# Attention's last group of a two-layer diffusion block: context tokens first, four output weights rounded ahead, and pieces of the output projection between scores and transposes

## The chip, the core and the metric

The kernel runs on one core of one Trainium2 chip. A core has a tensor engine (PE, matrix products), a vector engine (DVE), a scalar engine (ACT), GpSimd (POOL) and a queue for transfers (SP). Each engine takes its own instructions in order and waits on semaphores for the others. The metric is the time of one execution on the device in microseconds (us); smaller is better.

## The reference

Two layers work on 512 latent tokens (`x`) and 256 context tokens (`ctx`), width 1024. Layer 0 is windowed attention with 16 query heads in 4 groups that share one key and value head each; layer 1 is a bidirectional retention. Each layer is an adaLN-modulated mixer with a gated residual, followed by a SwiGLU feed-forward part with its own modulation. Only layer 0's attention and what follows it at once matter here:

```python
mx = split(silu(c) @ ada_w + ada_b, 6)            # adaLN: shift, scale, gate, twice
h = modulate(rms_norm(x, norm1_g), mx[0], mx[1])
q, k, v = split(h @ w_qkv)                        # QK-norm, 2-D rotary positions
# latent queries: 128-token blocks, keys of their window (|i - j| <= 128) and all context keys
# context queries: context keys only; a learned sink logit joins every softmax
p = softmax(concat([s_ctx, s_loc, sink]))
out = (p @ v) @ w_o                               # the output projection
x = x + mx[2] * out
x = x + mx[5] * swiglu(modulate(rms_norm(x, norm2_g), mx[3], mx[4]), w_in, w_out)
```

The context tokens go through the same weights with their own modulation.

## The kernel before

**Number format.** Every large product is made of three: a weight or activation is split into a rounded part (`hi`, made by ACT) and a remainder (`lo`, made by DVE), and `mm3` (line 144) issues hi x hi, lo x hi and hi x lo at lines 148, 149 and 150. A weight tile is loaded raw (128 x 1024, 512 KB) by `w_raw` (line 120) and split by `next_w` (line 136): ACT's rounding is line 140, DVE's remainder line 141. There are two raw tiles; a load waits until a split has emptied one. `w_parts` (line 126) chooses the room for the parts: two pairs in the pool `rp`, further ones in a pool of the stage.

**Attention.** Tokens stand in columns, features in rows. For each group g of 0 to 3 the loop at line 787 calls `attend` (line 736) for six blocks: four latent blocks of 128 queries, (0, 0) to (0, 3), and two context blocks, (1, 0) and (1, 1). A latent block sees 4 or 5 key tiles of 128 (window and context), a context block 2, so that a group has 22 key tiles. A block has three steps:

- `score`, for each of 4 heads: score products on PE (line 684) into one of three PSUM banks (`pS`), masked maximum on DVE (line 685), the exponential on ACT (line 101, two heads at a time), the reciprocal on DVE (line 695), the scaling of the probabilities on POOL (line 698).
- `turn`, for each key tile: four transposes on PE (line 707, one for each head) and a copy to SBUF by ACT or DVE in turn (line 709). It needs the probabilities of all four heads.
- `output`: value products on PE (line 719). In groups 0 to 2 the result is kept and split later (`split_o`); in group 3 ACT and DVE split it at once (lines 165, 166) into `o_t`, the operand of the output projection. Tile k of `o_t` holds heads 2k and 2k + 1, so a group gives two of eight k-tiles.

Between the blocks of groups 0 to 2 the query projection of the next group is made (`make_q`).

**Output projection.** The loop at line 810 has two halves of four output tiles (d). In a half four weights are split, then the four latent tiles (512 columns, 24 products each) and the four context tiles (256 columns, 24 products) are made in the two projection banks (`pj`). Behind each tile stand a gated add into the residual on DVE (`gated_add`, line 253) and the square for the second norm on ACT (line 207 or 209), added up by DVE (line 210). `ada_tile` (lines 263 to 273) makes one output tile of the adaLN modulation on DVE: a 512 KB load by SP and one multiply-and-reduce for each stream (line 271) against the condition row (`crow`, loaded and put through SiLU once at lines 255 to 261). Eight of them, `WO_ADA`, stand behind the latent tiles 0 to 6 and the context tile 2; the second norm's scale and shift (`fold_gain`, line 847) need them all. The second latent norm's sums (`rms(0)`) stand behind context tile 4, and `latent_shape` (line 861; DVE lines 866 and 868) makes the feed-forward operands. `first_two` (line 930) makes the first feed-forward tiles: gate (X) and up (Y) products of 384 columns, 24 each.

**What sets the order.** The lines above give the order in which instructions are recorded. A planner then lays them out for each engine by its own costs and by what is ready, so a later product may stand ahead of an earlier one on PE. In the program that it makes of this kernel, all 48 products of the latent output tiles 0 and 1 stand ahead of the last value products, the first 36 of them between the scores of group 2's context blocks and those of group 3's block (0, 2), the other 12 after the latent blocks. From the last value products on the planner keeps nearly the recorded order.

Of the kernel before, what the change touches and what calls it, by code (L numbers as in the profile page):

```python
# [9 lines left out]
F32R = mybir.dt.float32r  # L10
# [4 lines left out]
P = 128  # L15
D = 1024
KT = D // P
# [4 lines left out]
NKV = 4  # L22
# [3 lines left out]
RH = 4  # L26
EPS = 1e-6
UNITS = (4, 5, 8, 6)
WO_ADA = [(0, d) for d in range(7)] + [(1, 2)]
SPLIT_AT = (2, 4)  # L30
HALVES = (slice(0, 256), slice(256, 512))

# [17 lines left out]
def dit_kernel(ctx, tc, xT, cT, crow, small, consts, masks, tabs0, tabs1, jtab, adaQ, adaN, adaT, wst, out):  # L50
# [3 lines left out]
    NTOK = (SX, SC)  # L54
# [63 lines left out]
    wpos, wsel, ring = [0], [0], []  # L118

    def w_raw(pool=None, bufs=2):  # L120
        raw = T(pool or rp, 1024, "wraw", bufs)
        nc.sync.dma_start(raw, wst[wpos[0]])
        wpos[0] += 1
        return raw
# [11 lines left out]
    def next_w(pool, own=2, raw=None):  # L136

        raw = raw or w_raw()
        hi, lo = w_parts(pool, own)
        nc.scalar.copy(hi, raw)  # L140
        nc.vector.tensor_tensor(lo, raw, hi, op=sub)  # L141
        return hi, lo
# [9 lines left out]
    def project(w, hs, o):  # L152
        for k in range(KT):
            mm3(o, (w[0][:, k * P:(k + 1) * P], w[1][:, k * P:(k + 1) * P]), hs[k], k == 0, k == KT - 1)
# [47 lines left out]
    def add_square(s, k, t, c=slice(None), eng=nc.vector, tmp=t_sq, fresh=True):  # L202

        if k == 0:
            if fresh:
                ssq[s] = t_y(s)
            return nc.scalar.activation(ssq[s][:, c], t[:, c], AF.Square)
        sq = tmp(NTOK[s])[:, c]
        ins = nc.scalar.activation(sq, t[:, c], AF.Square)
        eng.tensor_tensor(ssq[s][:, c], ssq[s][:, c], sq, op=add)  # L210
        return ins

    def rms(s, c=slice(None), bank=pj, behind=()):
        y = ssq[s][:, c]
        n = y.shape[1]
        tot = bank()[:, :n]
        after(nc.tensor.matmul(tot, ones, y, start=True, stop=True), behind)
        neg_half_rstd(y, t_sq(n), tot, D)
# [33 lines left out]
    def gated_add(s, l, part, d, o, res):  # L252
        return nc.vector.scalar_tensor_tensor(res[d], o, mods[l, s][:, part, d:d + 1], res[d], mult, add)  # L253

    def cond_rows(pool):

        cr = T(pool, 2048, "crow", 1)
        nc.sync.dma_start(cr, crow.broadcast_to([P, 2048]))
        for i in range(2):
            silu(cr[:, i * 1024:(i + 1) * 1024], cr[:, i * 1024:(i + 1) * 1024])  # L260
        return cr

    def ada_tile(l, part, d, streams, cr, behind, room, w=None):

        j = part * 8 + d
        if w is None:
            w = T(room, 1024, "adaw", 1 if l else 3)
        (nc.gpsimd if l else nc.sync).dma_start(w, adaT[l, j])  # L268
        for s in streams:
            junk = T(rp, 1024, "y0", 1, BF16) if l else T(room, 1024, "junk", 1, BF16)  # L270
            after(nc.vector.tensor_tensor_reduce(junk, w, cr[:, s * 1024:(s + 1) * 1024], 1.0,  # L271
                                                 sm_t[:, C_ADAB + l * 48 + j:C_ADAB + l * 48 + j + 1], mult, add,
                                                 mods[l, s][:, part, d:d + 1]), behind)
# [86 lines left out]
    akv = AK.enter_context(tc.tile_pool(name="akv", bufs=1, reuse_waits="tile"))  # L360
# [279 lines left out]
        vt.append(v)  # L640
    psS.close()
    psA2 = At.enter_context(tc.tile_pool(name="psA2", bufs=1, reuse_waits="tile", space=PSUM))
    pS = lambda: T(psA2, 512, "S2", 3)

    run_dep = mybir.DependencyInfo(mybir.DependencyClass.Sync, mybir.DependencyReason.DATA)
    o_raw = {}
# [86 lines left out]
            dst = o_raw[g, s, b // 2].rearrange("p (e b q) -> p e b q", e=2, b=2)[:, :, b % 2, :]  # L733
            nc.vector.tensor_copy(dst, O.rearrange("p (e q) -> p e q", e=2))

    def attend(g, s, b):
        blk = Block(g, s, b)
        for i in range(4):
            blk.score(i)
        for ki in range(len(blk.keys)):  # L740
            blk.turn(ki)
        blk.output()

    def split_o(g):
        for e in range(2):
            hi, lo = t_h(0), t_h(0)
            for bp in range(2):
                cs = slice(bp * 256, bp * 256 + 256)
                split(o_raw[g, 0, bp][:, e * 256:e * 256 + 256], hi[:, cs], lo[:, cs])
            o_t[0][2 * g + e] = (hi, lo)  # L750
            oc = t_h(1)
            split(o_raw[g, 1, 0][:, e * 256:e * 256 + 256], oc[:, 0:SC], oc[:, SC:])
            o_t[1][2 * g + e] = (oc[:, 0:SC], oc[:, SC:])
# [30 lines left out]
    nc.vector.tensor_scalar(dcol[:, 2, :], lg[:, 4:8], 384.0, None, op0=mult)  # L784
    nc.vector.tensor_scalar(dcol[:, 3, :], lg[:, 4:8], -1.0, None, op0=mult)

    for g in range(NKV):
        for i, (s, b) in enumerate(((0, 0), (0, 1), (0, 2), (0, 3), (1, 0), (1, 1))):
            attend(g, s, b)
            if g < NKV - 1 and i in (1, 3):  # L790
                for piece in make_q(2 * g + 2 + i // 3):
                    piece()
            if (g, i) == SPLIT_AT:
                split_o(0)
                split_o(1)
        if g == 2:
            split_o(2)
    xr = load_stream(0)
    cres = load_stream(1)
    At.close()  # L800
    AK.close()
    PLAIN, ADA_FROM = 2, 4
# [2 lines left out]
    E = ExitStack()  # L805
    ep = E.enter_context(tc.tile_pool(name="ep", bufs=1, reuse_waits="tile"))
    wo_p = A.enter_context(tc.tile_pool(name="wo", bufs=1, reuse_waits="tile"))
    wsel[0] = 0
    ada_wo = [(part, d) for part in (3, 4) for d in range(4, KT)]
    for d4 in range(0, KT, 4):  # L810
        w = [next_w(wo_p) for _ in range(4)]
        if d4 == 0:
            cr = cond_rows(wo_p)
        for s, res in ((0, xr), (1, cres)):
            for d in range(d4, d4 + 4):
                o = pj(NTOK[s])
                project(w[d - d4], o_t[s], o)
                ins = gated_add(s, 0, 2, d, o, res)
                add_square(s, d, res[d])
                if (s, d) in WO_ADA:  # L820
                    ada_tile(0, *ada_wo.pop(0), (0, 1), cr, [ins], wo_p)
                if s == 1 and d == 4:
                    ln_exp_turn()
                    rms(0)
    assert not ada_wo
    A.close()

# [963 lines left out]
```

## Time and profile before

| | us |
|---|---|
| median of 3 runs | 1777.0 (1774.48 to 1779.74) |
| the profiled execution | 1777.24, its span 1775.5 |
| PE busy in the span | 1717.1 (97%) |
| DVE, ACT, POOL busy | 1356.0, 841.2, 134.4 |
| from the first score of group 0 to the first of group 3 | 103.1 to 268.6 |
| group 3 to its last value products | 268.6 to 325.3 |
| output projection, first feed-forward product | to 387.0 |

The profile is of one execution. Times in its rows are from the span's start. PE, PEld, DVE, ACT and POOL are the engines' busy times, PEld being PE's weight loads; PEclk is the granted clock of PE as a share of the full one. In a timeline row stand the start, the length, the engine, the line, the operation, output<-inputs by the program's names, and in brackets the idle time before it and what ended it. A product's length includes its way through the array; products that follow each other overlap, and their starts tell the rate. Some product records are missing in the trace.

### The profile page before, as it was taken

The numbers are of one execution on the slowest core, as the hardware profiler recorded it, in microseconds if no ns is written. First come the engines' busy times: TensorE is split into PE (matmuls) and PEld (weight loads), VectorE is DVE, ScalarE is ACT, GpSimd is POOL, SyncE is SP. The second block draws the span as 40 slices with busy tenths as digits, with TensorE's granted clock in tenths as the row PEclk, the third lists the DMA queues.
The fourth block names the chain that finished last, engine by engine and source line by source line (L and its number), as shares of the span: only waits on it lengthen the run. The fifth ranks groups of instructions, "written<-read, shape, count | busy, mean of one in ns | idle before, by whom it ended". The sixth has DMA issues, their size and how long they took to land.

```text
span 1775.5 us, 27602 instructions
## 1 busy us (share of the span) xinstructions
PE 1717.1 (97%) x10852; PEld 1527.1 (86%) x10852; DVE 1356.0 (76%) x2365; ACT 841.2 (47%) x1477; POOL 134.4 (8%) x275
## 2 busy tenths in 40 slices
PE   6899999999999999999998999999999999999999
PEld 4777776789999999999978788898897899999998
DVE  6697786788778778777789758758758798777774
ACT  5477676456333434242465534524524564445432
POOL 0035344100000000000010000000000000000000
PEclk9999999999999999999999999999999999999999
DMA  8610002434243534343342534434433323333222
GB/s 334 239 36 25 25 1 84 145 107 165 73 154 107 157 116 143 119 146 111 123 133 88 164 106 132 153 102 132 153 104 119 95 72 116 94 112 107 92 88 83
DMA packets 59891, 206.68 MB, mean 116 GB/s; under 512 B 6641, under 2 KB 7025, under 8 KB 59505
## 3 DMA queue, kind: packets, MB, share of 16 engines
q1 hardware_dynamic: 52848, 179.75, 31.2%
q0 software_dynamic: 6912, 25.17, 4.8%
q8 instruction: 85, 1.39, 0.3%
q14 instruction: 46, 0.37, 0.1%
HBM read 202.80 MB, written 2.10 MB: 115 GB/s over the span
## 4 chain that ended last, share of the span: by engine, by line
PE 74%; DVE 13%; ACT 4%; DMA 4%; issue 2%; POOL 2%; SPq 0%; ACTq 0%; DVEq 0%; POOLq 0%
PE Y L835 13%; PE Z L835 6%; PE pj L148 6%; PE pj L150 6%; PE pj L149 6%; PE Y L1180 4%; PE Z L1193 3%; PE X L835 3%; DVE wlo L166 3%; DMA wraw<-in_wst_dram 2%; PE pT L707 2%; PE S L684 2%; PE pO L719 2%; PE pj L1193 2%; PE X L1180 1%
## 5 line engine op out<-in xcount | busy, mean ns | idle before, releaser
L165 ACT CAST whi<-wraw 128x1024 fp32r<-128x1024 f32 x177 | 185.5, 1051 | 305.3 <-PE Z L150 71.5
L166 DVE TENSOR_TENSOR wlo<-wraw,whi 128x1024 fp32r<-128x1024 f32 x177 | 215.7, 1221 | 42.1 <-ACT whi L165 41.6
L835 PE MATMUL Y<-aq,whi 128*128 128x384 f32 x640 | 173.7, 335 | 0.9 <-ACT hn L973 0.8
L253 DVE SCALAR_TENSOR_TENSOR res<-pj,mod,res 128x512 f32<-128x512 f32 (+1 forms) x112 | 81.6, 729 | 70.3 <-PE pj L150 69.1
L141 DVE TENSOR_TENSOR wlo<-wraw,whi 128x1024 fp32r<-128x1024 f32 x80 | 97.9, 1223 | 36.6 <-ACT whi L140 36.0
L140 ACT CAST whi<-wraw 128x1024 fp32r<-128x1024 f32 x80 | 84.0, 1050 | 75.9 <-DMA wraw<-in_wst_dram 26.8
L835 PEld LDWEIGHTS Y<-aq,whi 128*128 128x128 f32 x640 | 116.6, 188 | 2.4 <-ACT hn L973 2.0
L271 DVE CUSTOM_DVE_ANT_0 y<-adaw,crow,small_sb 128x1024 bf16<-128x1024 f32 x64 | 81.9, 1279 | 33.7 <-DMA adaw<-in_adaT_dram 33.5
L835 PE MATMUL Y<-aq,wlo 128*128 128x384 f32 x320 | 107.0, 334 | 0.0
L101 ACT ACTIVATE pr<-pr,stat,qs 128x513 f32<-128x513 f32 (+2 forms) x96 | 74.2, 775 | 30.7 <-DVE stat L691 29.8
L1193 PE MATMUL Z<-whi,sA 128*128 128x512 f32 x256 | 81.0, 392 | 0.6 <-ACT whi L165 0.6
L698 POOL TENSOR_SCALAR pr<-pr,stat 128x512 f32<-128x512 f32 (+2 forms) x96 | 68.0, 721 | 86.7 <-DVE stat L695 66.6
L148 PE MATMUL pj<-ax,whi 128*128 128x512 f32 x176 | 68.7, 390 | 1.0 <-DVE res L253 1.0
L150 PE MATMUL pj<-ax,whi 128*128 128x512 f32 x176 | 68.6, 390 | 0.0
L149 PE MATMUL pj<-ax,wlo 128*128 128x512 f32 x176 | 68.5, 389 | 0.0
L707 PE MATMUL pT<-const_sb,pr 128*128 128x128 f32 x352 | 58.0, 284 | 10.9 <-POOL pr L698 8.6
L148 PE MATMUL pj<-act,whi 128*128 128x512 f32 x168 | 66.0, 393 | 0.1
L149 PE MATMUL pj<-act,wlo 128*128 128x512 f32 x168 | 65.9, 392 | 0.0
L707 PEld LDWEIGHTS pT<-const_sb,pr 128*128 128x128 f32 x352 | 38.8, 140 | 31.3 <-POOL pr L698 19.2
L150 PE MATMUL pj<-act,whi 128*128 128x512 f32 x168 | 65.5, 390 | 0.0
L268 POOL DMA_DIRECT2D adaw<-in_adaT_dram x48 | 25.6, 533 | 520.6 <-DVE mod L271 420.8
L685 DVE CUSTOM_DVE_ANT_0 pr<-S,mask,qs 128x256 f32<-128x256 f32 (+1 forms) x96 | 53.1, 567 | 14.3 <-PE S L684 7.9
(518 smaller groups left out, 5273.7 us busy)
## 6 DMA issues: line engine op xcount, KB each, us to landing
wraw<-in_wst_dram SPq DMA_DIRECT2D x238, 512.0 KB, 3.6
adaw<-in_adaT_dram POOLq DMA_DIRECT2D x48, 512.0 KB, 3.9
wx<-in_wst_dram SPq DMA_DIRECT2D x24, 512.0 KB, 4.6
adan<-in_adaQ_dram SPq DMA_DIRECT2D x16, 512.0 KB, 8.0
adan<-in_adaN_dram SPq DMA_DIRECT2D x16, 512.0 KB, 8.5
res<-in_xT_dram SPq DMA_DIRECT2D x16, 256.0 KB, 5.5
adaw<-in_adaT_dram SPq DMA_DIRECT2D x8, 512.0 KB, 4.0
aq<-in_adaN_dram SPq DMA_DIRECT2D x12, 256.0 KB, 6.4
```

The costliest lines, as they stand in the source:

```text
L140: nc.scalar.copy(hi, raw)
L141: nc.vector.tensor_tensor(lo, raw, hi, op=sub)
L148: nc.tensor.matmul(o, whi, xhi, start=first, stop=False)
L149: nc.tensor.matmul(o, wlo, xhi, start=False, stop=False)
L150: return nc.tensor.matmul(o, whi, xlo, start=False, stop=last)
L165: nc.scalar.copy(hi, t)
L166: return nc.vector.tensor_tensor(lo, t, hi, op=sub)
L271: after(nc.vector.tensor_tensor_reduce(junk, w, cr[:, s * 1024:(s + 1) * 1024], 1.0, sm_t[:, C_ADAB + l * 48 + j:C_ADAB + l * 48 + j + 1], ...
L707: nc.tensor.transpose(tp[:, a * P:(a + 1) * P], self.pr[(0, 2, 1, 3)[a]][:, ki * P:(ki + 1) * P], ident)
L835: nc.tensor.matmul(o, p, r, start=first and k + i == 0, stop=k == 3 and i == 2, skip_group_check=not first)
L1180: ins = nc.tensor.matmul(o[:, e * SC:(e + 1) * SC], p[:, ws], r, start=first and k + e + i == 0, stop=k == 3 and i == 2, skip_group_check= ...
L1193: ins = nc.tensor.matmul(o, p, r, start=first and k + i == 0, stop=k == 3 and i == 2, skip_group_check=not first)
```

## The change

1. In group 3 the two context blocks come first, then the four latent blocks.
2. `attend` takes pieces of work: the first is recorded between a block's scores and its transposes, the second between its transposes and its value products. In group 3 they are pieces of the output projection, `out_part(s, d, k0, k1)`: stream s, output tile d, k-tiles k0 to k1. Latent tiles 0, 1 and 2 get k-tiles 0 to 5 (the groups 0 to 2) early, and 6 and 7 after the last block. Context tiles 0 to 3 are made whole, since both context blocks are done by then. Context tile 3 and latent tile 2 take score banks.
3. Four output weights are split before group 3 in place of two: two in `rp`, one in the attention's own pool `ap`, and one by `key_room_w` in room that the keys of groups 0 and 1 leave, in two half-width splits.
4. After attention stand the latent tiles 3 to 7 and then the context tiles 4 to 7. The condition row is loaded after all eight weights are recorded. The eight adaLN tiles stand behind latent tiles 3 to 7, as 1, 2, 2, 2, 1.
5. The last four weights take the rooms `rp`, stage pool, stage pool, `rp`; before it was `rp`, `rp`, stage pool, stage pool in each half.

```diff
-WO_ADA = [(0, d) for d in range(7)] + [(1, 2)]
+WO_ORDER = [(0, d) for d in range(3, KT)] + [(1, d) for d in range(4, KT)]
+WO_ADA = {(0, 3): 1, (0, 4): 2, (0, 5): 2, (0, 6): 2, (0, 7): 1}
...
-    def attend(g, s, b):
+    def attend(g, s, b, *fills):
         blk = Block(g, s, b)
         for i in range(4):
             blk.score(i)
+        for f in fills[:1]:
+            f()
         for ki in range(len(blk.keys)):
             blk.turn(ki)
+        for f in fills[1:]:
+            f()
         blk.output()
...
-    for g in range(NKV):
-        for i, (s, b) in enumerate(((0, 0), (0, 1), (0, 2), (0, 3), (1, 0), (1, 1))):
+    latent, context = ([(s, b) for b in range(n)] for s, n in ((0, 4), (1, 2)))
+    for g in range(NKV - 1):
+        for i, (s, b) in enumerate(latent + context):
             attend(g, s, b)
...
+    split_o(2)
     xr = load_stream(0)
     cres = load_stream(1)
...
+    def key_room_w():
+
+        raw, hi, lo = w_raw(), [], []
+        for c in range(2):
+            hi.append(T(akv, 512, "k", 8, F32R))
+            lo.append(T(akv, 512, "k", 8, F32R))
+            split(raw[:, 512 * c:512 * c + 512], hi[c], lo[c])
+        return [(hi[k // 4][:, k % 4 * P:k % 4 * P + P], lo[k // 4][:, k % 4 * P:k % 4 * P + P]) for k in range(KT)]
+
+    wo = [cut(next_w(ap, 1)), cut(next_w(ap, 1)), key_room_w(), cut(next_w(ap, 1))]
+    begun = {}
+
+    def out_part(s, d, k0, k1, bank=pj):
+
+        if k0 == 0:
+            begun[s, d] = bank(NTOK[s])
+        for k in range(k0, k1):
+            mm3(begun[s, d], wo[d][k], o_t[s][k], k == 0, k == KT - 1)
+        if k1 < KT:
+            return None
+        ins = gated_add(s, 0, 2, d, begun[s, d], streams[s][1])
+        add_square(s, d, streams[s][1][d])
+        return ins
+
+    early = [(0, 0, 0, 3), (0, 0, 3, 6), (1, 0, 0, KT), (1, 1, 0, KT), (1, 2, 0, KT), (0, 1, 0, 6)]
+    for (s, b), part in zip(context + latent, early):
+        fills = [lambda: out_part(*part)]
+        if (s, b) == latent[-1]:
+            fills.append(lambda: out_part(1, 3, 0, KT, pS))
+        attend(NKV - 1, s, b, *fills)
+    out_part(0, 2, 0, 6, pS)
+    for d in range(3):
+        out_part(0, d, 6, KT)
     At.close()
     AK.close()
...
-    wsel[0] = 0
     ada_wo = [(part, d) for part in (3, 4) for d in range(4, KT)]
-    for d4 in range(0, KT, 4):
-        w = [next_w(wo_p) for _ in range(4)]
-        if d4 == 0:
-            cr = cond_rows(wo_p)
-        for s, res in ((0, xr), (1, cres)):
-            for d in range(d4, d4 + 4):
-                o = pj(NTOK[s])
-                project(w[d - d4], o_t[s], o)
-                ins = gated_add(s, 0, 2, d, o, res)
-                add_square(s, d, res[d])
-                if (s, d) in WO_ADA:
-                    ada_tile(0, *ada_wo.pop(0), (0, 1), cr, [ins], wo_p)
-                if s == 1 and d == 4:
-                    ln_exp_turn()
-                    rms(0)
+    for wsel[0] in (0, 2, 3, 1):
+        wo.append(cut(next_w(wo_p)))
+    cr = cond_rows(wo_p)
+    for s, d in WO_ORDER:
+        ins = out_part(s, d, 0, KT)
+        for _ in range(WO_ADA.get((s, d), 0)):
+            ada_tile(0, *ada_wo.pop(0), (0, 1), cr, [ins], wo_p)
+        if (s, d) == (1, 4):
+            ln_exp_turn()
+            rms(0)
```

More of the change, by code (lines that the diff above doesn't have):

```diff
@@ L642, in dit_kernel @@
     psA2 = At.enter_context(tc.tile_pool(name="psA2", bufs=1, reuse_waits="tile", space=PSUM))
-    pS = lambda: T(psA2, 512, "S2", 3)
+    pS = lambda n=512: T(psA2, 512, "S2", 3)[:, :n]
     run_dep = mybir.DependencyInfo(mybir.DependencyClass.Sync, mybir.DependencyReason.DATA)
@@ L785, in dit_kernel @@
     nc.vector.tensor_scalar(dcol[:, 3, :], lg[:, 4:8], -1.0, None, op0=mult)
-    for g in range(NKV):
-        for i, (s, b) in enumerate(((0, 0), (0, 1), (0, 2), (0, 3), (1, 0), (1, 1))):
+    latent, context = ([(s, b) for b in range(n)] for s, n in ((0, 4), (1, 2)))
+    for g in range(NKV - 1):
+        for i, (s, b) in enumerate(latent + context):
             attend(g, s, b)
-            if g < NKV - 1 and i in (1, 3):
+            if i in (1, 3):
                 for piece in make_q(2 * g + 2 + i // 3):
@@ L795, in dit_kernel, with cut @@
                 split_o(1)
-        if g == 2:
-            split_o(2)
+    split_o(2)
     xr = load_stream(0)
     cres = load_stream(1)
+    streams = ((0, xr), (1, cres))
+    def cut(w):
+        return [tuple(t[:, k * P:(k + 1) * P] for t in w) for k in range(KT)]
+    def key_room_w():
[26 more added lines that the diff above has]
+        out_part(0, d, 6, KT)
     At.close()
```

## The prediction

> **What bounds the kernel now.** I read the page first, then the windows by stage, then the timeline of the tensor engine (PE) and of the vector engine (DVE) from the last attention group to the first feed-forward tile, and last the waits.
>
> ```profile
> PE 1717.1 (97%) x10852; PEld 1527.1 (86%) x10852; DVE 1356.0 (76%) x2365; ACT 841.2 (47%) x1477; POOL 134.4 (8%) x275
> core 0: us, PE busy (x) PEld busy (x) DVE busy (x) ACT busy (x) POOL busy (x), PEclk, DMA share, GB/s
> 103.10:268.60 165.50, 158.33 (x1108) 125.82 (x1106) 134.35 (x410) 117.26 (x272) 67.64 (x141) 1.00 0.06 17
> 268.60:294.90 26.30, 24.80 (x158) 18.54 (x157) 19.80 (x71) 15.46 (x40) 12.11 (x27) 1.00 0.40 141
> 280.00:290.00 10.00, 9.88 (x64) 7.28 (x63) 6.99 (x28) 6.35 (x16) 3.53 (x9) 1.00 0.38 139
> 294.90:325.30 30.40, 26.05 (x177) 17.25 (x175) 17.80 (x61) 18.79 (x49) 11.27 (x29) 1.00 0.12 44
> 325.30:333.40 8.10, 6.50 (x15) 4.76 (x15) 4.14 (x6) 6.89 (x8) 0.00 (x0) 0.58 0.80 291
> 333.40:374.20 40.80, 40.80 (x227) 35.72 (x226) 32.41 (x53) 8.74 (x13) 0.00 (x0) 1.00 0.39 117
> ```
>
> PE bounds the whole. The rows by stage are groups 0 to 2 of attention; the last group with pieces of the output projection among it (to 294.9) and without (to 325.3); the hand-over, where the granted clock is 0.58; the projection. PE counts as busy while it waits for short dependent work, so I also work out useful time: number of instructions in the program's order times the distance between their starts.
>
> ```profile
> 268.60 0.48 PE L684 MATMUL S<-k,q 128*128 128x256 f32 x2
> 311.99 1.09 PE L707 MATMUL pT<-const_sb,pr 128*128 128x128 f32 x8 [0.33 <-ACT tt L709]
> 314.05 1.95 PE L719 MATMUL pO<-tt,v 128*64 128x256 f32 x16
> 315.93 1.47 PE L707 MATMUL pT<-const_sb,pr 128*128 128x128 f32 x7
> 340.23 0.39 PE L150 MATMUL pj<-h,whi 128*128 128x512 f32 x1
> 340.46 0.39 PE L148 MATMUL pj<-h,whi 128*128 128x512 f32 x1
> 342.32 0.28 PE L149 MATMUL pj<-hc,wlo 128*128 128x256 f32 x1
> 342.43 0.28 PE L150 MATMUL pj<-hc,whi 128*128 128x256 f32 x1
> 387.03 0.34 PE L148 MATMUL X<-aq,whi 128*128 128x384 f32 x1
> 387.38 0.33 PE L150 MATMUL X<-aq,whi 128*128 128x384 f32 x1
> 400.32 0.34 PE L150 MATMUL X<-aq,whi 128*128 128x384 f32 x1
> ```
>
> So a 512-column product takes 0.2275 (over a longer stretch), 256 columns 0.118, 384 columns 0.35 / 2 = 0.174; a transpose (1.09 - 0.28) / 7 = 0.115; a pair of value products 1.88 / 8 = 0.234. Scores are taken like the others by width. From the first score of group 3 (268.6) to its last value product (325.3) the order has 64 + 16 scores, 102 transposes, 52 value pairs and 45 latent projection products: 7.5 + 2.8 + 11.7 + 12.2 + 10.2 = 44.4 us useful in 56.7, or 78%. Groups 0 to 2, filled with the query projection, come to 139 of 165.5 (84%). Counted the same way from its records, 280 to 290 gives 9.1 of 10, and a few records are missing there: about 93%.
>
> **The hand-over.**
>
> ```profile
> 324.20 1.08 PE L719 MATMUL pO<-tt,v 128*64 128x256 f32 x8 [0.88 <-ACT sq L209]
> 326.59 0.80 PE L148 MATMUL pj<-h,whi 128*128 128x512 f32 x1 [1.30 <-ACT whi L140]
> 328.29 0.63 PE L149 MATMUL pj<-h,wlo 128*128 128x512 f32 x1
> 328.72 0.63 PE L150 MATMUL pj<-h,whi 128*128 128x512 f32 x1
> ```
>
> After the last value products PE waits for a weight's rounding, then runs at half clock: 0.43 between starts in place of 0.2275, until 333.4. The rest of the projection after 325.3 is 144 latent and 192 context products, 32.8 + 22.6 = 55.4 us; but the first feed-forward product starts at 387.0, 61.7 after 325.3. Hence 6.3 us are lost, nearly all in the hand-over.
>
> **The change, part by part.** Call T the end of the last group's value products (325.3 before).
>
> 1. *Pieces between scores and transposes.* Before, two latent output tiles (48 products, 10.9 us) were done ahead of T, put there by the planner. Now it is three fourths of three latent tiles, two of them ahead of T (36 products, 8.2), and four context tiles (96, 11.3): 19.5 us. So 8.6 us more useful work stands before T; useful time from 268.6 to T becomes 53.0. At 84% it takes 63.1 us, at 93% 57.0. I take 59 (90%), nearer the stretch 280 to 290, since it has the same filler; groups 0 to 2 also carried the query chain, which has no counterpart here. T comes 2.3 us later (0.3 to 6.4). The latent tile begun first holds one of the two projection banks to the end, so the context tiles take turns in the other, each behind the gated add of the one before (0.48 and its place on DVE); the order puts scores or transposes between them, so I take 0, and up to 1 us for each of three without that cover, which lies inside the range above. POOL scales the same tiles in another order, and on SP the fifth raw weight goes ahead of the residual loads, which the context tiles need only late in the group: 0 for both.
>
> 2. *Four weights ahead.* Before, the third and fourth were rounded at the hand-over. One now goes into freed key room in two half-width splits, early in group 2. They add what the row at 348.93 below has, 1.2 us of DVE and about as much ACT, to a stretch where DVE is busy 134.35 of 165.50. Between 0 (DVE gaps take them) and 1.3; I take 0.3. The fourth moves into group 3.
>
> 3. *The hand-over.* The 6.3 us go: after the last value products stand 18 products of a latent tile that need nothing of that block (4.1 us), which cover its rounding. If that cover failed, the 1.30 gap and 2.9 us of half clock (14 products at 0.2 more) would be back. From T, PE's own list is 156 latent and 96 context products plus the sums for the latent norm, 35.5 + 11.3 + 0.6 = 47.4 us.
>
> 4. *What is late next: DVE.* The projection after T gets shorter by 14 us but keeps all eight adaLN tiles (two DVE operations each); before, DVE was busy 32.41 of 40.80 in the projection's full-speed stretch.
>
> ```profile
> 341.34 0.75 DVE L253 SCALAR_TENSOR_TENSOR res<-pj,mod,res 128x512 f32<-128x512 f32 x1
> 342.01 1.27 DVE L271 CUSTOM_DVE_ANT_0 junk<-adaw,crow,small_sb 128x1024 bf16<-128x1024 f32 x1
> 343.21 0.08 DVE L271 DVE_READ_ACCUMULATOR2_ANT mod<- 128x1 f32 x1
> 343.21 0.68 DVE L210 TENSOR_TENSOR y<-y,sq 128x512 f32<-128x512 f32 x1
> 343.81 1.28 DVE L271 CUSTOM_DVE_ANT_0 junk<-adaw,crow,small_sb 128x1024 bf16<-128x1024 f32 x1
> ...
> 348.93 1.22 DVE L141 TENSOR_TENSOR wlo<-wraw,whi 128x1024 fp32r<-128x1024 f32 x1
> 350.07 0.48 DVE L253 SCALAR_TENSOR_TENSOR res<-pj,mod,res 128x256 f32<-128x256 f32 x1
> 350.46 1.27 DVE L271 CUSTOM_DVE_ANT_0 junk<-adaw,crow,small_sb 128x1024 bf16<-128x1024 f32 x1
> ...
> 383.60 0.74 DVE L866 SCALAR_TENSOR_TENSOR act<-res,acol,y 128x512 f32<-128x512 f32 x1
> ...
> 385.80 1.14 DVE L868 SCALAR_TENSOR_TENSOR aq<-act,mod,aq 128x384 fp32r<-128x384 f32 x2
> ```
>
> By starts: gated add 0.67 (context 0.39), adaLN operation 1.21, square 0.60 (context about half), weight remainder 1.14, norm product 0.67, its remainder 0.53. In the new order DVE has, from the gated add of latent tile 3 to the first norm product: 5 gated adds, 16 adaLN operations, 5 squares, 3 remainders, 3 context gated adds with 2 squares, and the norm's four small ones: 3.4 + 19.4 + 3.0 + 3.4 + 1.8 + 1.5 = 32.5 us. It cannot start before that tile is done, T + 13.9 on PE's list, and about 1.5 us goes in waits: the condition row's transfer now waits for the second output weight's last use (T + 6.7) and lands after the 4.7 us it took before,
>
> ```profile
> 320.73 0.33 SPq L258 DMA_DIRECT2D crow<-in_crow_dram  x1
> DMA to landing us min/median/max: 4.7/4.7/4.7
> ```
>
> and on SP the raw weights 6 and 7 and the adaLN tiles stand behind it; on ACT the row's two activations and the roundings of weights 6 and 7 are interleaved. So the first norm product runs at T + 48. Before it ran at 383.60, T + 58.3, with 3.4 us of PE's context tiles still to come. Eight products, eight remainders and 2.2 us of other work follow: the last operand is there at T + 59.7. The second feed-forward weight now reuses the room of the last output weight, free only when PE has finished, so the order has the 24 gate products first, each three waiting for a new operand, and 23 up products (4.0 us) after them; then 24 of the next tile (4.2) and the context sums (0.4): T + 68.6. Before, gate and up went in pairs and this point was passed at 400.4 (the 400.32 row), T + 75.1. The step gives 6.5 us in place of the 14.8 that PE's list alone would give.
>
> Sum: 2.3 + 0.3 - 6.5 = -3.9 us against the profiled execution's 1777.2, that is 1773.3; the median, 1777.0, lies 0.2 under that execution. With the bounds of steps 1 and 2 and 2 us either way for DVE's waits, this case spans 1769 to 1780.
>
> **Rivals.**
>
> *DVE keeps up.* If the adaLN operations fall into waits I count twice, or the last group is dense enough that PE waits less for DVE, half or all of the 8.3 us in step 4 comes back: 1769 down to 1765. For it: in 333.4 to 374.2 DVE had 8.4 us free. Against: its new list has 32.5 us of work in about 34.
>
> *The clock halves at the first feed-forward tile.* Three 0.174 products per 1.2 us of DVE keep PE thin for 9 us, like this later place:
>
> ```profile
> 944.00:948.00 4.00, 2.32 (x9) 2.03 (x10) 4.00 (x5) 1.56 (x3) 0.00 (x0) 0.54 0.09 36
> ```
>
> At half clock for the 6.8 us seen at the hand-over, half of it exposed in useful time, it costs up to 3.4: 1776.7. [...]
>
> *Slower: the pieces stand in series with the softmax chain.* PE takes its queue in order, so a piece between scores and transposes delays transposes that are ready.
>
> ```profile
> POOL pr L698 <- DVE stat L695: 12.7, 6, 3.6
> ```
>
> By the waits of 294.9 to 325.3 (us in total, times, longest) POOL's scaling of the probabilities, and what precedes it, paces that stretch. If each piece adds its whole length, and the context tiles' gated adds and squares (2.6 us) delay DVE's reductions too, T comes 8.6 + 2.6 later and the key split costs its 1.3: 11.2 + 1.3 - 6.5 = +6.0, 1783.2. It ends slower once the last group takes over 62.9 us. Against: 280 to 290 has pieces among scores and PE busy 9.88.
>
> **How the numbers follow.** Forecast case 0.40, DVE keeps up 0.25, clock 0.13, series 0.22. A measurement can tell about 0.3%, 5.3 us, from no change: faster is below 1771.7, slower above 1782.3. Faster takes DVE-keeps-up and two fifths of the forecast case (0.41); slower most of the series case (0.18); the rest is 0.41. Range 1763 to 1784; the forecast case's own is 1769 to 1780.
>
> **What would show it.** Right: granted clock 1.00 at the hand-over and no wait of a projection product for a weight rounding; last score-to-value stretch of 57 to 63 us; DVE without gaps from the third latent gated add to the norm; gate products in threes a microsecond apart. Wrong: up products paired with gate products from the start, or transposes waiting for POOL in the last group as long as before.

## The result, and the profile after

The changed kernel takes 1773.9 us (median of 20 runs, 1770.2 to 1776.8) where the kernel before, beside it, takes 1777.0 (20 runs, 1774.5 to 1779.7). The ratio is 0.9979, 95% interval 0.9973 to 0.9986: 2.5 to 4.8 us less. The forecast was 1773.3. The profiled execution spans 1773.1 us, against 1775.5.

The windows by stage of the changed kernel answer to those shown of before (busy time of PE, of its weight loads, of DVE, ACT and POOL, then the granted clock and the DMA share); the last two rows are single stretches at half clock. Group 3's first score, at 268.60 before, stands at 267.65 here.

```profile
core 0: us, PE busy (x) PEld busy (x) DVE busy (x) ACT busy (x) POOL busy (x), PEclk, DMA share, GB/s
102.40:268.60 166.20, 160.79 (x1114) 128.83 (x1112) 135.01 (x420) 119.77 (x277) 70.01 (x143) 0.99 0.12 38
268.60:327.94 59.34, 56.72 (x409) 44.26 (x409) 37.51 (x129) 33.83 (x86) 23.39 (x54) 1.00 0.09 23
327.94:341.80 13.86, 13.86 (x62) 11.49 (x62) 6.30 (x9) 6.62 (x10) 0.00 (x0) 1.00 0.41 148
341.80:376.68 34.88, 34.07 (x194) 29.27 (x193) 34.23 (x57) 11.88 (x18) 0.00 (x0) 1.00 0.50 164
376.68:395.82 19.14, 16.87 (x79) 14.44 (x78) 17.41 (x32) 17.67 (x31) 0.00 (x0) 0.91 0.44 146
382.80:386.20 3.40, 3.38 (x11) 2.87 (x11) 3.40 (x6) 3.40 (x7) 0.00 (x0) 0.50 0.00 0
236.00:239.40 3.40, 3.40 (x15) 3.10 (x16) 2.52 (x7) 2.17 (x7) 0.00 (x0) 0.50 0.00 0
```

The stretch from 268.6 to the last value products, 56.7 us before, now takes 59.3, with PE busy nearly throughout, and the hand-over has the whole clock. But in the 34.88 us that follow, DVE is busy 34.23: it has become the full engine. The timeline of PE shows the hand-over: the value products end at 327.94 (this is T now), and the next latent products follow at once.

```profile
326.00 1.95 PE L720 MATMUL pO<-tt,v 128*64 128x256 f32 x16
327.87 0.50 PE L149 MATMUL S<-h,k 128*128 128x512 f32 x1
328.21 0.40 PE L150 MATMUL S<-h,k 128*128 128x512 f32 x1
328.45 0.39 PE L151 MATMUL S<-h,k 128*128 128x512 f32 x1
```

The timeline of DVE from the gated add of latent tile 3 to the last operand of the first feed-forward tile:

```profile
341.81 0.75 DVE L254 SCALAR_TENSOR_TENSOR res<-pj,mod,res 128x512 f32<-128x512 f32 x1 [2.00 <-PE pj L151]
342.81 2.47 DVE L142 TENSOR_TENSOR wlo<-wraw,whi 128x1024 fp32r<-128x1024 f32 x2 [0.26 <-ACT whi L141]
345.20 1.28 DVE L272 CUSTOM_DVE_ANT_0 junk<-adaw,crow,small_sb 128x1024 bf16<-128x1024 f32 x1
...
375.21 0.74 DVE L903 SCALAR_TENSOR_TENSOR act<-res,acol,y 128x512 f32<-128x512 f32 x1
...
385.34 1.22 DVE L142 TENSOR_TENSOR wlo<-wraw,whi 128x1024 fp32r<-128x1024 f32 x1
386.47 0.62 DVE L905 SCALAR_TENSOR_TENSOR aq<-act,mod,aq 128x384 fp32r<-128x384 f32 x1
```

From 342.81, where the weight remainders start after a wait of 0.26 us, to 375.21 there is one wait more, of 0.26 us too. The first norm product stands at T + 47.3, the last operand is there at 387.09, T + 59.1. On PE the gate products (X) wait for these operands, and all up products (Y) but one, which needs only the rounded parts and runs at 377.98, begin the moment the second weight's remainder (385.34 + 1.22) is there:

```profile
376.68 0.41 PE L149 MATMUL X<-aq,whi 128*128 128x384 f32 x1
...
381.38 0.44 PE L149 MATMUL X<-aq,whi 128*128 128x384 f32 x1 [0.69 <-ACT aq L904]
...
382.56 0.54 PE L151 MATMUL X<-aq,whi 128*128 128x384 f32 x1 [0.56 <-DVE aq L905]
...
383.75 0.69 PE L151 MATMUL X<-aq,whi 128*128 128x384 f32 x1
...
386.35 0.34 PE L150 MATMUL X<-aq,wlo 128*128 128x384 f32 x1
386.61 0.45 PE L150 MATMUL Y<-aq,wlo 128*128 128x384 f32 x1
...
395.82 0.33 PE L149 MATMUL Y<-aq,whi 128*128 128x384 f32 x1
```

The 395.82 row is where the second half of the tokens begins, T + 67.9; before it was passed at 400.4, T + 75.1.

| Place (from T, us) | before | forecast | after |
| --- | --- | --- | --- |
| T itself, from the span's start | 325.3 | 327.9 | 327.9 |
| first norm product (DVE) | 58.3 | 48 | 47.3 |
| first feed-forward product (PE) | 61.7 | | 48.7 |
| last latent operand (DVE) | | 59.7 | 59.1 |
| second token half begins | 75.1 | 68.6 | 67.9 |
| first context add behind the feed-forward part | 118.2 | | 110.0 |

The last row (the gated add that reads `Z`, at 443.54 before and 437.90 now) is the mark by which the executions below are compared, since from there on all kernels do the same. The mark moved by -5.6 us, or -4.9 counted from each execution's first score (103.1 and 102.4). By the end 2.3 us remain in this pair: among others, the changed kernel's execution is at half clock for 6.83 us from 1393.1, the other for 3.41 from 1398.3, at a place that the change doesn't touch. The mean granted clock differs between executions of one kernel, 0.991 to 0.997 over the 20 of the changed one, so the median difference is the number for the whole and the mark the one for the place.

### The profile page after: what moved, and what is told of

Read it like the earlier page. It is cut to its first block, busy times and chain, and to the rows that moved or that the text cites. A ratio compares the mean times of both kernels' runs of the same rounds, so it can differ in the third digit from the quotient of the medians.

```text
span 1773.1 us, 27606 instructions
## 1 busy us (share of the span) xinstructions
PE 1720.2 (97%) x10852; PEld 1532.8 (86%) x10852; DVE 1354.4 (76%) x2366; ACT 842.5 (48%) x1478; POOL 136.8 (8%) x275
## 4 chain that ended last, share of the span: by engine, by line
PE 77%; DVE 12%; DMA 4%; ACT 3%; issue 2%; POOL 2%; SPq 0%; ACTq 0%; DVEq 0%; POOLq 0%
PE Y L872 14%; PE Z L872 7%; PE pj L151 6%; PE pj L150 6%; PE pj L149 6%; PE Z L1230 4%; PE X L872 3%; DMA wraw<-in_wst_dram 3%; DVE wlo L167 2%; PE pT L708 2%; PE Y L1217 2%; PE pj L1230 2%; PE S L685 2%; PE pO L720 2%; PE X L1217 1%
```

## The experiments

Theory: from T on, DVE's adaLN work sets when the first feed-forward tile ends. Rivals: something else is late there; the pieces carry or don't carry the gain; the room or the record of the second feed-forward weight decides why its products come last.

### More and less adaLN work on DVE

```diff
-            ada_tile(0, *ada_wo.pop(0), (0, 1), cr, [ins], wo_p)
+            ada_tile(0, *ada_wo.pop(0), (0, 1)[:1 + len(ada_wo) % 2], cr, [ins], wo_p)     # ada_4less
+            ada_tile(0, *ada_wo.pop(0), (0,), cr, [ins], wo_p)                             # ada_8less
+            ada_tile(0, *ada_wo.pop(0), (0, 1, 1)[:2 + len(ada_wo) % 2], cr, [ins], wo_p)  # ada_4more
```

> The changed kernel, with the adaLN operation of the context stream left out for four of the eight adaLN tiles behind the output projection (those columns are set to zero, so the context tokens' second modulation is not computed there); all eight 512 KB transfers stay. Theory (DVE sets when the first feed-forward tile ends): four operations of 1.21 us fewer, so the first norm product stands 4.8 us earlier from the last value product (about 42.5 in place of 47.3) and the second token half of the first feed-forward tile starts 4.8 us earlier from it (63 in place of 67.9); median about 4.8 under the changed kernel's 1773.9, 1769. Rival (something else is late, the transfers or PE's own list): less than 1 us of gain, 1773 to 1774.

> The changed kernel, with the context stream's adaLN operation left out for all eight of those tiles (columns set to zero, as above); the transfers stay. Theory: DVE is relieved of 9.7 us; PE's own list after the last value product (47.4 us to the first feed-forward product, 60 to the second token half) becomes the bound after about 8 of them, gate and up products run in pairs or without waits and the clock is not halved there: median 8 to 9 us under the changed kernel, 1765 to 1766. Rival (DVE only looks full): no more than 2 us, 1772 or above. If the gain goes on in step (9.7 or more), PE's list was not the next bound.

> The changed kernel with the adaLN operation of the context stream done twice for four of the eight tiles (the same result is written again): 4.8 us more DVE work in the stretch before the norm. Theory (DVE sets it, no slack): the first norm product comes 4.8 us later from the last value product, 52.1 in place of 47.3, and the median is 4 to 5 us over the changed kernel's, 1778 to 1779. Rival (DVE has slack there): 0 to 2 us over it.

| kernel | median (runs) | ratio to before, 95% | first norm product | first X | mark |
| --- | --- | --- | --- | --- | --- |
| changed kernel | 1773.9 (20) | 0.9979 [0.9973, 0.9986] | T + 47.3 | T + 48.7 | T + 110.0 |
| ada_4less | 1767.9 (6) | 0.9944 [0.9926, 0.9961] | T + 43.7 | T + 48.0 | T + 106.8 |
| ada_8less | 1768.3 (6) | 0.9943 [0.9928, 0.9959] | T + 43.7 | T + 48.1 | T + 106.8 |
| ada_4more | 1777.9 (12) | 0.9997 [0.9987, 1.0007] | T + 53.1 | T + 54.6 | T + 114.9 |

In ada_4less and ada_8less four and eight operations of the context stream are left out, and the columns that they would have made are zero. Four operations more cost 5.8 us at the norm, 4.9 at the mark and 4.1 in the median (4.8 by count): DVE has no slack. Four fewer return 3.6 us at the norm and 3.2 at the mark, where 4.8 were expected, and four more left out return nothing further, where 8 to 9 were. So by the mark DVE's adaLN work holds back 3.2 us, not 8.3. The median of ada_4less falls by more, 6.0 us. Its profiled execution isn't halved near 236, where the changed kernel's is, and has T at 326.89 in place of 327.94; whether that accounts for the rest was not shown. What comes next is visible in ada_8less, in its timelines of DVE and PE:

```profile
368.21 0.69 DVE L198 SCALAR_TENSOR_TENSOR sq<-pj,sq 128x512 f32<-128x512 f32 x1 [0.67 <-ACT sq L197]
...
370.14 2.07 DVE L904 SCALAR_TENSOR_TENSOR act<-res,acol,y 128x512 f32<-128x512 f32 x3
...
380.16 1.22 DVE L142 TENSOR_TENSOR wlo<-wraw,whi 128x1024 fp32r<-128x1024 f32 x1
```

```profile
374.51 0.34 PE L149 MATMUL X<-aq,whi 128*128 128x384 f32 x1
...
380.36 0.44 PE L149 MATMUL X<-aq,whi 128*128 128x384 f32 x1 [0.95 <-ACT aq L905]
381.43 0.44 PE L150 MATMUL Y<-aq,wlo 128*128 128x384 f32 x1 [0.45 <-DVE wlo L142]
```

DVE now waits for ACT in the norm's own chain, and PE's list reaches the first X at T + 48.1 (47.4 forecast). But the up products still start only with the weight's remainder, which stands behind 14 of the 16 norm operations: the second token half begins at 391.16, T + 64.7, where PE's list alone would have had T + 60.3 (47.4, then 72 products of 0.174 and the context sums).

### Why the up products come last: the room or the record

```diff
-    for wsel[0] in (0, 2, 3, 1):
+    for wsel[0] in range(4):                          # rooms, rooms_ws
...
+    w01 = [next_w(fp, 1), next_w(fp, 1)]              # ws, rooms_ws
     latent_shape()
-    first = first_two([next_w(fp, 1), next_w(fp, 1)], [next_w(fp, 1), spare_w()])
+    first = first_two(w01, [next_w(fp, 1), spare_w()])
```

> The changed kernel with only the rooms of the last four output weights changed, 0, 1, 2, 3 in place of 0, 2, 3, 1; all work is done. If, as step 4 of the prediction has it, the room of the second feed-forward weight is why the gate products come first, then its split can be done some 7 us before the projection ends and up products fill the gaps: 3 to 4 us less, 1770 to 1771. Rival (the split of that weight is recorded behind the norm products, so DVE makes its remainder late in any room): up products still start behind the last gate product, 1773 to 1775.

> The changed kernel with its own rooms, and only the record of the first two feed-forward weights' splits moved ahead of the norm products; all work is done. If the room decides, PE or DVE now waits in order for the end of the last context tile and the split behind it (ACT 1.05, DVE 1.22): no gain, or up to 2 us more, 1774 to 1776. Rival (the recorded place decides): up products stand among the gate products, the second token half starts 2 to 4 us earlier from the last value product than in the changed kernel (67.9), no half clock there, median 1770 to 1772.

> The changed kernel with the last four output weights put in the rooms 0, 1, 2, 3 in place of 0, 2, 3, 1, and the first two feed-forward weights split ahead of the norm products in the recorded order; all work is done. The second feed-forward weight then takes a room that is free some 7 us before the projection ends. Theory: up products run among the gate products in DVE's gaps, 23 of them (4.0 us) no longer stand behind the last operand, and PE is dense enough that its clock stays whole (0.8 us or so): the second token half starts 3 to 4.5 us earlier from the last value product, median 1769.5 to 1771. Rival (the up weight's remainder, 1.14 us of DVE, now stands ahead of the norm products, and pairs wait as gates did): 0 to +1, 1774 to 1775.

rooms took 1774.6 us, ratio 0.9987 [0.9973, 1.0000], mark at T + 112.8: no gain, and in its profiled execution a loss of 2.9 us at the mark, with half clock from 368.3 and from 382.0. ws took 1771.7, 0.9963 [0.9950, 0.9976], mark at T + 108.1. rooms_ws took 1770.8, 0.9957 [0.9941, 0.9972], mark at T + 109.5. In rooms the room is free early, and yet DVE makes the remainder last, because it is recorded behind the norm; the first product that needs it waits. The timeline of DVE in rooms, and then that of PE:

```profile
385.80 1.67 DVE L905 SCALAR_TENSOR_TENSOR aq<-act,mod,aq 128x384 fp32r<-128x384 f32 x3
387.39 2.35 DVE L142 TENSOR_TENSOR wlo<-wraw,whi 128x1024 fp32r<-128x1024 f32 x2
```

```profile
387.63 0.34 PE L151 MATMUL X<-aq,whi 128*128 128x384 f32 x1
388.66 0.44 PE L150 MATMUL Y<-aq,wlo 128*128 128x384 f32 x1 [0.69 <-DVE wlo L142]
```

In ws, with the late room, the remainder stands between the third and fourth norm product, and up products fill PE from 378.63, T + 52.3, on. The timeline of DVE in ws, and then that of PE:

```profile
376.36 0.75 DVE L903 SCALAR_TENSOR_TENSOR act<-res,acol,y 128x512 f32<-128x512 f32 x1
...
377.36 1.22 DVE L142 TENSOR_TENSOR wlo<-wraw,whi 128x1024 fp32r<-128x1024 f32 x1
```

```profile
378.63 0.44 PE L150 MATMUL Y<-aq,wlo 128*128 128x384 f32 x1 [0.65 <-DVE wlo L142]
378.91 0.34 PE L151 MATMUL Y<-aq,whi 128*128 128x384 f32 x1
```

So the record decides and the room does not. The gain at the mark is 1.9 us, just under the 2 to 4 that were expected at the second token half: the remainder now delays the norm operations behind it by its own 1.14. In rooms_ws it even comes ahead of the first of them, which goes to T + 50.4 (that execution is also at half clock from 369.0). There the median came out as expected, 3.0 us under the changed kernel's, but the mark moved by only 0.5, so the expected step is not shown to be the cause. Near 370 rooms is halved too (its context products start 0.21 us apart up to 371.7), and ws and crow_ws, with the late room, are not (0.11 apart); why was not tested.

### Relief for DVE by POOL

```diff
-        add_square(s, d, streams[s][1][d])
+        add_square(s, d, streams[s][1][d], eng=nc.gpsimd if s == 0 else nc.vector)
```

> The kernel rooms_ws with the seven sums of squares of the latent tiles moved from DVE (0.60 each) to POOL, which is idle there; all work is done. In rooms_ws the first norm product came 50.4 us after the last value product, the norm's own chain allows 43.7 (ada_8less). Theory (DVE's time sets it): five or six of the moved sums lie in that stretch, 3.0 to 3.6 us, so the norm starts at 46.8 to 47.4, the first feed-forward product at about 48.5 to 49, and the median falls by 3 us below rooms_ws, to 1767 to 1768.5. Rival (POOL's sum takes longer than DVE's and stands in the norm's chain, or slows DVE while both run): 0 to -1, 1770 to 1771.

It took 1777.7 us, 0.9997 [0.9983, 1.0010]: 7 us more than rooms_ws, the first norm product at T + 53.2 in place of 50.4. The theory's direction is wrong here; the rival named the reason, but not the size (0 to -1 us). The timeline of POOL in this kernel, and then that of DVE:

```profile
350.18 1.47 POOL L211 TENSOR_TENSOR y<-y,sq 128x512 f32<-128x512 f32 x1 [3.82 <-ACT sq L210]
356.62 1.47 POOL L211 TENSOR_TENSOR y<-y,sq 128x512 f32<-128x512 f32 x1 [4.96 <-ACT sq L210]
```

```profile
349.23 1.27 DVE L272 CUSTOM_DVE_ANT_0 junk<-adaw,crow,small_sb 128x1024 bf16<-128x1024 f32 x1
350.55 2.19 DVE L272 CUSTOM_DVE_ANT_0 junk<-adaw,crow,small_sb 128x1024 bf16<-128x1024 f32 x1
...
355.67 1.27 DVE L272 CUSTOM_DVE_ANT_0 junk<-adaw,crow,small_sb 128x1024 bf16<-128x1024 f32 x1
356.98 2.19 DVE L272 CUSTOM_DVE_ANT_0 junk<-adaw,crow,small_sb 128x1024 bf16<-128x1024 f32 x1
```

An adaLN operation that starts beside a sum on POOL takes 2.19 us in place of 1.27, and ends 1.08 after the end of POOL's sum (351.65 and 358.09): it lost 0.92 of the 1.10 us for which the two overlap, nearly all of it. Moving a sum of 0.60 off DVE cost DVE 0.9. The other half of the rival, POOL's sum in the norm's chain, is there too: PE waits 4.72 us for the last of the latent sums before its products for the norm at 370.30, where in rooms_ws it waits 1.2 for DVE's. How much of the 7 us each makes was not separated.

### The pieces

no_pieces records the whole output projection behind the last value products. Two further kernels give DVE an earlier start in it and in ws: four adaLN tiles without an order behind a tile (no_pieces_ada), and the condition row in another room together with the edit of ws (crow_ws, no_pieces_crow_ws). The last two record two adaLN tiles behind the sixth output weight; behind latent tiles 3 to 6 then stand 1, 2, 2 and 1. In no_pieces_ada the four free ones stand behind the condition row, and one each behind latent tiles 3 to 6.

```diff
-    early = [(0, 0, 0, 3), (0, 0, 3, 6), (1, 0, 0, KT), (1, 1, 0, KT), (1, 2, 0, KT), (0, 1, 0, 6)]
...
+    for s, b in context + latent:                     # no_pieces
+        attend(NKV - 1, s, b)
+    for d in range(3):
+        out_part(0, d, 0, KT)
+    for d in range(4):
+        out_part(1, d, 0, KT)
...
-    for wsel[0] in (0, 2, 3, 1):                      # crow_ws, no_pieces_crow_ws
-        wo.append(cut(next_w(wo_p)))
-    cr = cond_rows(wo_p)
+    raws = [w_raw(), w_raw(), None, None]
+    cr = cond_rows(wo_p)
+    for wsel[0], raw in zip((0, 2, 3, 1), raws):
+        wo.append(cut(next_w(wo_p, raw=raw)))
+        if len(wo) == 6:
+            for _ in range(2):
+                ada_tile(0, *ada_wo.pop(0), (0, 1), cr, [], wo_p)
```

> The changed kernel without pieces between scores and transposes: context first and four weights ahead as in it, but all of the output projection recorded behind the last value products (the planner may still move some of it ahead). Theory: the last value product comes about 15 us earlier (34 to 40 us useful at 78% from the first score of group 3), PE's list after it grows by up to 19.5 us, and DVE's adaLN work now fits beside it, so that gate and up products are not late: the second token half starts within 3 us of the changed kernel's place, either side, median 1771 to 1777. So the pieces are worth little as long as DVE is late behind them. Rival (the pieces carry the gain): the whole difference of the fill, 0.22 of 19.5 us and more, is lost: 1778 or above.

> The kernel no_pieces with four of the eight adaLN tiles allowed as soon as the condition row is there, in place of behind latent tile 3 (which in that order comes 25 us after the last value product); all work is done. Theory (the loss of no_pieces was DVE's adaLN work starting late, not the missing fill): DVE's work starts some 5 us earlier or more, the first norm product comes at most at 52 from the last value product in place of 57.4, and the time falls by 4 to 6 us, to 1774 to 1776, near the changed kernel. Rival (the fill itself is the gain): no change beyond 1 us, 1779 to 1781.

> The kernel ws with the condition row in a room that the last block's probabilities leave (before the last value product) in place of that of the second output weight, and the first two adaLN tiles allowed as soon as it is there; all work is done. Theory (DVE's adaLN work starts late because the row lands late): in the changed kernel the row was issued 6.9 us after the last value product and the first adaLN operation came at 17.3 from it; here the row can be issued about at that product, so three to four operations (3.6 to 4.9 us) fall into time in which DVE was idle. The first norm product then comes at 43.7 to 45 from the last value product (47.4 in ws), the first feed-forward product at 48, and the median falls to 1768 to 1770. Rival (the tiles' transfers or the two activations of the row, put earlier, hold up the weights or the gated adds): no gain, 1771 to 1774.

> The kernel no_pieces with both edits of crow_ws (second feed-forward weight recorded ahead of the norm products, condition row early); all work is done. It prices the pieces where DVE is not late. Theory: last value product at 322 as in no_pieces, PE's list from there 132 latent and 192 context products and the sums, 30.0 + 22.6 + 0.6 = 53.2 us, so the first feed-forward product at about 375.5, some 1 us behind crow_ws: the pieces are worth 0 to 2 us, and most of what no_pieces lost (6.3 us) was DVE's late start. Rival (the fill is the gain): 5 us or more over crow_ws.

| kernel | median (runs) | ratio to before, 95% | first score to T | first norm product | first X | mark |
| --- | --- | --- | --- | --- | --- | --- |
| before | 1777.0 (20) | 1 | 222.2 | T + 58.3 | T + 61.7 | T + 118.2 |
| no_pieces | 1780.2 (12) | 1.0009 [0.9997, 1.0021] | 219.3 | T + 57.4 | T + 60.5 | T + 121.1 |
| no_pieces_ada | 1778.5 (11) | 0.9998 [0.9987, 1.0009] | 220.6 | T + 56.1 | T + 60.7 | T + 119.9 |
| no_pieces_crow_ws | 1775.9 (11) | 0.9987 [0.9978, 0.9996] | 220.7 | T + 55.4 | T + 59.9 | T + 116.4 |
| crow_ws | 1769.4 (5) | 0.9950 [0.9938, 0.9962] | 224.1 | T + 46.3 | T + 49.3 | T + 107.6 |

The values 220.6 and 220.7 contain a window at half clock near 236, which the other three executions don't have. The pairs of rows below are the last value products and the first X product, first of no_pieces_crow_ws, then of crow_ws:

```profile
321.00 1.95 PE L720 MATMUL pO<-tt,v 128*64 128x256 f32 x16 [0.78 <-DVE tt L710]
...
382.89 0.34 PE L149 MATMUL X<-aq,whi 128*128 128x384 f32 x1
```

```profile
325.49 1.95 PE L720 MATMUL pO<-tt,v 128*64 128x256 f32 x16
...
376.76 0.34 PE L149 MATMUL X<-aq,whi 128*128 128x384 f32 x1
```

My theory on the pieces falls, and the rival ("the fill is the gain") holds: without pieces the same kernel is 5 to 7 us slower (ratios 1.0009 against 0.9979, and 0.9987 against 0.9950; medians 1780.2 against 1773.9, and 1775.9 against 1769.4). In both orders 156 latent products stand behind T, since the planner puts 36 of them ahead of it without being told to; I had counted 132. What the pieces move ahead of T is the 96 context products, 11.3 us. They put T only about 5 us later (219.3 against 224.1; the 15 us that I expected were far off), since they lie largely in gaps in which PE waited for the softmax chain: its waits in the last group add up to 6.6 us in no_pieces and to 2.0 in the changed kernel. That leaves 6 us. That the loss without them is DVE's late start is ruled out by no_pieces_crow_ws: between T and its first X, PE is busy 59.22 of 59.95 us with 156 latent and 192 context products, so that its own list sets the time there.

The kernel without pieces also shows what the rest of the change is worth without them: the weights ahead, the order of the blocks and of the output tiles, the rooms and the later adaLN tiles, with 12 latent products (2.7 us) behind T and not ahead of it. It has no half clock at the hand-over (1.00 from 322.15 to 333), its first X comes 4.4 us earlier than before (382.65 against 387.03), and it is no faster: its mark from the first score is 340.3, that of before 340.4. The first feed-forward tile gives all of it back, with gate products that wait for DVE and up products behind them. The hand-over by itself was not priced, since these parts were not taken apart.

no_pieces_ada settled nothing: the condition row still lay in the room of the second output weight, and was issued at 338.63, 14.5 us after T; its norm came 1.3 us earlier, not 5. crow_ws is the fastest kernel of the study with all work done, 0.4 to 0.6% under before, but its step by itself gave little: the norm at T + 46.3 (ws: 47.4) and not 43.7 to 45, the mark 0.4 us earlier than in ws. The row was issued at 323.35 and there at 328.2 (4.9 us), but ACT put it through SiLU behind two squares, and DVE did the first adaLN operation behind the gated add of latent tile 3, as in the changed kernel. The timeline of ACT in crow_ws, and then that of DVE:

```profile
336.15 1.35 ACT L210 ACTIVATE sq<-res 128x512 f32<-128x512 f32 x2 [0.48 <-DVE res L254]
337.52 1.28 ACT L108 ACT_TABLE_LOAD   x1
338.81 2.01 ACT L108 ACTIVATE crow<-crow 128x1024 f32<-128x1024 f32 x2
```

```profile
341.30 0.75 DVE L254 SCALAR_TENSOR_TENSOR res<-pj,mod,res 128x512 f32<-128x512 f32 x1 [2.00 <-PE pj L151]
341.97 1.28 DVE L272 CUSTOM_DVE_ANT_0 junk<-adaw,crow,small_sb 128x1024 bf16<-128x1024 f32 x1
```

Whether another order on ACT and DVE would bring the rest was not tried.

## Why the prediction was right or wrong

**The time.** 1773.3 against 1773.9; the result lies in the forecast case, faster by 0.2%. The sum of -3.9 us stands beside -4.9 at the mark and -3.1 (2.5 to 4.8) in the median. The mechanism as a whole was right; one step had a wrong cause and two wrong sizes inside it. That the total came within 0.6 us is partly luck: without the half-clock window at 236, T would stand 2.0 us later than before, counted from the first score, and not 2.6; from T on the changed kernel gains 7.2 us up to the second token half and 8.3 up to the mark, and not 6.5; and behind the mark this pair of executions loses 3.3 us that the sum doesn't contain.

**Step 1, the pieces.** Right in the main: 59 us for the last group, and 60.3 measured from its first score (267.65) to T; T at 327.9, measured 327.94. Counted from the first score of group 0, T moved by 3.3 us, of which 1.3 is the half-clock window at 236 (executions without it have 224.1 to 224.3, the changed kernel's 225.5). The density came near the 90% that was taken from the stretch 280 to 290: by the same prices the products recorded in those 60.3 us make 52.4 useful, 87%. The planner put six latent products of the pieces ahead of the group's first score. The sign of being wrong that the prediction named for this step nearly came: transposes wait 2.0 us for POOL in the last group, 2.7 before. PE's other waits there (2.6 us before) are what is gone.

**Step 2, the split in key room.** Its 0.3 us was not measured by itself; it lies inside the T above.

**Step 3, the hand-over.** Right as an event: no wait of a projection product for a rounding, clock 1.00. In no_pieces it is repaired too, and nothing of it is left at the mark; its 6.3 us were not measured by themselves.

**Step 4, DVE late next.** The places were right to 0.7 us (norm T + 48 against 47.3, last operand 59.7 against 59.1, second half 68.6 against 67.9; the terms that the prediction lists for this last one add up to 68.3), and ada_4more confirms that DVE has no slack. The share was wrong. The text put all 8.3 us between PE's list and DVE's down to DVE; of these the adaLN work holds 3.2 by the mark, and then the norm's own chain is next, at T + 43.7. The rest hangs on the sentence "the second feed-forward weight now reuses the room of the last output weight, free only when PE has finished, so the order has the 24 gate products first". Its effect was as forecast (one up product ran early, 23 came last), but the room is not its cause: an early room brought no gain, an early record did.

**The rivals.** *DVE keeps up* did not happen. *The clock halves at the first feed-forward tile* did, from 382.8 for 3.41 us, and cost nothing in that execution: the last of the waiting gate products started at 386.35, and the up products could not start before the remainder was done at 386.56. The price of up to 3.4 us was too high, because the stretch was waiting for DVE at either clock. The gaps ahead of it were short: the largest marked in the 6 us before is 0.71; at the hand-over of the kernel before, gaps of 0.88 and 1.30 stand ahead of the half clock. *Pieces in series with the softmax chain* did not happen: the 96 context products, 11.3 us, put T only about 5 us later.

## What to carry to other kernels

A stall that is removed from the bounding engine is worth only what the engine next in line can follow: count that engine's list to the same place, and then look for the third bound behind it, since relief stops there (here 3.2 of 8.3 us). Filler between dependent steps pays by the idle time that it covers, here about 6 of 11.3 us, and an order that a planner makes has to be read from the program before a piece is counted as moved. When the products of two weights are to alternate, look at where the second weight's preparation is recorded on the engine that makes it, and not only at its room.

## What the runs showed of the hardware

- In rooms_sq_ws the sums on POOL and the work of DVE don't run beside each other for free: an adaLN operation of 1.27 us takes 2.16 to 2.19 beside a sum on POOL (1.45 to 1.48), at each of four places, and two weight remainders take 3.45 beside a sum of 1.70, where two at 377.70, beside none, take 2.35.
- In the profiled executions of the kernel before and of the changed one half clock begins on a grid and lasts one or two steps of it: 3.41 or 6.83 us for every window that ends inside the kernel. The starts in the changed kernel's execution (48.3, 236.0, 382.8) lie 55 and 43 steps of 3.413 us apart. It came after gaps far shorter than a step: in rooms from 382.0, after gaps of 0.57 and, across its start, 1.30; in the kernel before from 326.5, after 0.88 and, across its start, 1.30; in the changed kernel from 382.8, after 0.69 and 0.56. From 236 to 240 the granted clock is 0.57 in the changed kernel and 1.00 in the kernel before, with PE busy 3.13 and 2.85 of the 4 us ahead; what makes it halve was not settled.
- One such window near 236, where PE is otherwise busy, costs 1.3 us (225.5 from the first score to T, against 224.1 to 224.3); the one at 382.8 in the changed kernel, where PE waits for DVE, costs nothing (last waiting gate product at 386.35, remainder done at 386.56). Between the profiled executions of the kernel before and the changed one the difference moves by 3.3 us behind the mark, from -5.6 to -2.3, where the two do the same work: as much as the change itself is worth.
